# A mixing projection in which some rounded parts of the next operand are stored one or two products later

## The chip, the cores and the metric

The kernel runs on one core of one Trainium2 chip. The metric is the device time of one execution in microseconds (us). Work is spread over five engines, each with its own in-order list of instructions: TensorE (PE in the profile; PEld is its weight load), VectorE (DVE), ScalarE (ACT), GpSimd (POOL) and SyncE (SP). POOL and SP here mostly issue DMA transfers, each through a queue of its own. Times of single instructions are given from the start of the profiled span.

## The reference

One layer of a decoder trunk, 512 tokens by 2048 features, in float32. Cut to the part around the change:

```
merged = gc * conv_branch + ga * attn_branch
x = x + merged @ w_mix_out                  # mixing projection, 2048 x 2048
h = rmsnorm(x, g_mlp)                       # the second norm
u = square(relu(h @ w_ff1))                 # 2048 x 8192
x = x + u @ w_ff2                           # 8192 x 2048
out = rmsnorm(x, g_final)
```

## The kernel before

**How a product is made.** A float32 operand is rounded to a high half (`split`, line 111, ACT, into tile `th`) and a low half, which is the rest (line 114, DVE, into `tl`). Each of `th` and `tl` has two buffers. A product is then three passes on PE: high by high, low by high and high by low (lines 195, 197, 199 in `mm_rows` for the mixing projection, lines 171, 175, 177 in `mm_cols` for the MLP). One product is 16 + 8 + 16 + 8 = 48 matmuls in the mixing projection.

**Groups.** `w_mix_out` is worked through in four groups of 512 columns (g = 0 to 3, called first to fourth here), then `w_ff1` in sixteen groups, of which the first is `g0`. Each group is a two-by-two block product done with seven products instead of eight. They are named by the block or the sum of blocks of the left operand: A11, A12, S1, S3, S2, S4, A22. Sums and differences of weight blocks are made by DVE (line 128). Weights (tiles `x`) come by 1 MB loads (line 234): SP issues those of the mixing projection, POOL those of `g0`. The order of products is A11, A12, S1, S3, S2, S4, A22 in the first three groups (`head`, `tail2`) and A11, A12, S1, S2, S4, S3, A22 in the fourth (`tail3`). PE accumulates into banks a, b, c and d; ACT copies a bank out as it fills (`snap`, line 268, `o`) and DVE adds the others (`plus`, line 131).

**What follows a group.** Each group yields four quarters `o` of the new x. DVE adds the old x to a quarter (line 1372, tile `xr`), POOL stores it (line 1373, `x_d`), ACT sums its squares (line 532, `junk`), PE transposes it in four matmuls (line 1389, `ptr`), and ACT copies the transposed pieces, scaled by the gain, into `f` (line 1398). There is one pair of `f` tiles, which each group uses in turn; so a group can write it only when the group before it has stored what lies there.

**The five parts.** From the `f` of one group the kernel makes five pieces of the left operand of `w_ff1`: the sums S1, S2, S3 and S4 and the plain block A22. Each has the name of a product of the MLP that will read it; here they are called part S1 and so on. `Mix.give` calls `out`, which rounds one part: high half into one of two buffers `staged` (line 111, ACT), low half in place in `f` or `s` (line 114, DVE). POOL then stores both halves to DRAM (line 1414, `h_d`, 256 KB each). Blocks A11 and A12 take another way (`f_d`, line 1401); their halves are made by `split_part` after a load (line 1349) in one instruction of 1536 columns on ACT and one on DVE, tile `A`. Parts of the fourth group do not leave the core. Before `g0` needs them the stored parts are loaded again (line 1347, `S` and the last `A`, 1.5 MB each, on POOL).

**What sets the order.** A table, `after`, says behind which product of the running group each step for the group before it is written. The parts S2 and S4 are given at once when the sums are made (`sums`), S1, S3 and A22 by the table. The build then orders each engine's list from that; instructions marked to be kept in program order, the rounding and the stores of the parts among them, keep the order in which they were written. The lines of the table are 1527 to 1546:

```
        late = g == 1
        for n in ("A12", "S3") if late else ("A11", "S2" if g == 3 else "S1"):
            after.add(n, turn_waiting)
        after.add("A22", turn_first)
        if before:
            after.add("A12" if late else "A11", before.first_of, before.sums)
            for n, part in (("A12", "S1"), ("S1", "S3"), ("S2", "A22")):
                after.add(n, lambda before=before, part=part: before.give(part))
        ...
            after.add("S4", lambda: g0.ahead(0, 0))
            after.add("S4", lambda: split_part("A11"))
```

Of the kernel before, what the change touches and what calls it, by code (L numbers as in the profile page):

```python
# [45 lines left out]
def tile_hybrid_block(ctx: ExitStack, tc, x, g_mix, w_in, b_f, b_gate, conv_w, w_conv_out,  # L46
# [679 lines left out]
    part = stat.tile([P, 1], F32, tag="vf", name="part", bufs=4)  # L726
# [10 lines left out]
    A11, A12 = (Q1.cut(n, 0) for n in ("A11", "A12"))  # L737
# [24 lines left out]
    A11, A12 = (Q1.cut(n, 1) for n in ("A11", "A12"))  # L762
# [314 lines left out]
    n = 0  # L1077
# [252 lines left out]
    n = turns[0] + 1  # L1330
# [11 lines left out]
    def begin_part(n, k):  # L1342

        Q2[n] = pair(k, F32R, n).rearrange("p e (q s) -> p e q s", q=KT // 2)
        if n in SPLIT:
            tc.keep_in_program_order(
                nc.gpsimd.dma_start(out=Q2[n][:, :, :KT // 2 - 2].bitcast(F32), in_=h_d[:, SPLIT.index(n)]))
        else:
            nc.gpsimd.dma_start(out=Q2[n][:, 1, :KT // 2 - 2].bitcast(F32), in_=f_d[:, int(n == "A12")])

    def split_part(n):
        lo = Q2[n][:, 1, :KT // 2 - 2]
        split_in_order(lo.bitcast(F32), Q2[n][:, 0, :KT // 2 - 2], lo, kept=n)
# [164 lines left out]
    for g in range(4):  # L1518
        mix = mixes[g] = Mix(g)
        after = Steps()  # L1520
        if g == 0:
            for n, n2 in zip(("A11", "A12", "S1", "S3", "S2"), ("S1", "S3", "S2", "S4", "A22")):
                after.add(n, quads3[n2])
        if g == 3:
            after.add("S1", mix.fourth, lambda: begin_part("A12", 4))
# [3 lines that stand above are left out]
        after.add("A22", turn_first)  # L1529
        if before:  # L1530
            after.add("A12" if late else "A11", before.first_of, before.sums)
            for n, part in (("A12", "S1"), ("S1", "S3"), ("S2", "A22")):
                after.add(n, lambda before=before, part=part: before.give(part))
        if g < 3:
            after.add("S2", mix.fourth)
        else:
            after.add("A12", lambda: begin_part("A11", 0))
            after.add("S4", lambda: g0.ahead(0, 0))
            after.add("S4", lambda: split_part("A11"))
            after.add("S3", lambda: g0.ahead(1, 0))  # L1540
            after.add("A22", lambda: g0.ahead(0, 1))
            after.add("A22", lambda: split_part("A12"))
        group = groups[g]
        group.after = after
        if g == 0:
            after.add("A11", group.first_sum)
        if g == 3:
            group.mid["A22"] = turn_first
            group.freed = lambda: (g0.ahead(1, 1), begin_part("S1", 1))
        group.head(True, between=groups[1].first if g == 0 else lambda: None)  # L1550
        (group.tail2 if g < 3 else group.tail3)()
        before = mix
# [15 lines left out]
    def factors(common, r):  # L1568

        ms = const.tile([P, NT], F32, name="ms")  # L1570
        nc.vector.tensor_reduce(out=ms, in_=ss2, axis=AX.X, op=ALU.add)
        nc.gpsimd.tensor_tensor(out=r, in0=ms, in1=mhalf.to_broadcast([P, NT]), op=ALU.pow)
        ones = const.tile([P, P], F32, name="ones")
        nc.vector.memset(ones, 1.0 / S)
        pt = bank(6, "mean")
        nc.tensor.matmul(pt[:, :NT], ones, ms, start=True, stop=True)
        mean, back = (const.tile([P, 1], F32, name=n) for n in ("mean", "back"))
        nc.vector.tensor_reduce(out=mean, in_=pt[:, :NT], axis=AX.X, op=ALU.add)
        nc.gpsimd.tensor_tensor(out=common, in0=mean, in1=mhalf, op=ALU.pow)
        nc.vector.reciprocal(out=back, in_=common)  # L1580
        nc.vector.tensor_scalar(out=r, in0=r, scalar1=back, scalar2=None, op0=ALU.mult)
        nc.vector.tensor_tensor(out=r, in0=r, in1=r, op=ALU.mult)
# [5 lines left out]
                     A12=[in_order, lambda: mix.sums(False), lambda: factors(common, turned)])  # L1588
# [250 lines left out]
```

## Time and profile before

| | |
|---|---|
| time, median of 3 runs | 2417.17 us (2416.66 to 2418.52) |
| profiled execution, its own time | 2418.55 us |
| span in the profile | 2416.7 us |
| mean granted TensorE clock | 0.998 |
| PE busy | 2396.0 us, 99% of the span |
| DVE busy | 2029.8 us, 84% |
| ACT busy | 1205.1 us, 50% |
| POOL busy | 300.0 us, 12% |

A row of the timeline has the start, the length, the engine, the line, the operation, the tiles (out<-in, buffer numbers left out) and, in brackets, how long the engine stood idle before it and what ended that. The second group of the mixing projection runs from about 1059 to 1098 us, the fourth from about 1138 to 1181 us, and the first group of the MLP follows.

### The profile page before, as it was taken

What the parts mean: (1) busy time and instruction counts of PE and PEld (TensorE: products, weight loads), DVE (VectorE), ACT (ScalarE), POOL (GpSimd) and SP (SyncE); (2) the same over time, 40 slices, a digit from 0 to 9 for tenths busy, and PEclk for the clock granted to TensorE, in tenths of its full rate; (3) what the DMA queues carried; (4) which work ended last, traced back from release to release, by engine and by line L of the source; (5) the groups of instructions that cost most, each with busy time, mean ns of one, the idle gap of its engine ahead of it and who ended that gap; (6) DMA issues with size and microseconds to landing.
All of it is one profiled execution on the core that took longest, in us unless ns stands there. A gap on an engine that the chain in (4) does not pass through costs nothing.

```text
span 2416.7 us, 41351 instructions
## 1 busy us (share of the span) xinstructions
PE 2396.0 (99%) x17775; PEld 2259.7 (94%) x17775; DVE 2029.8 (84%) x1683; ACT 1205.1 (50%) x1238; POOL 300.0 (12%) x480
## 2 busy tenths in 40 slices
PE   9999999999999999999999999999999999999998
PEld 9999999999999999899999999999998888888886
DVE  7987677789888768888988889888887888889898
ACT  7444444445545534446665666666664333333334
POOL 1100111121111112023300000000011001100000
PEclk9999999999999999999999999999999999999999
DMA  8664444464565755566956564655678467665662
GB/s 276 187 189 153 150 154 153 153 205 152 178 201 181 259 176 202 179 193 224 324 184 225 199 231 170 224 206 198 233 288 292 168 210 252 218 212 183 232 231 100
DMA packets 279847, 491.98 MB, mean 204 GB/s; under 512 B 11820, under 2 KB 191112, under 8 KB 279280
## 3 DMA queue, kind: packets, MB, share of 16 engines
q1 hardware_dynamic: 226384, 272.71, 35.6%
q0 software_dynamic: 52672, 215.57, 24.4%
q8 instruction: 139, 2.28, 0.4%
q10 hardware_dynamic: 608, 1.06, 0.1%
q14 instruction: 44, 0.36, 0.0%
HBM read 379.70 MB, written 109.07 MB: 202 GB/s over the span
## 4 chain that ended last, share of the span: by engine, by line
PE 90%; DVE 3%; issue 2%; DMA 2%; ACT 1%; POOL 1%; SPq 0%; POOLq 0%; DVEq 0%; ACTq 0%
PE a L171 6%; PE a L175 6%; PE a L177 6%; PE d L171 5%; PE d L175 5%; PE d L177 5%; PE a L197 5%; PE a L195 5%; PE a L199 5%; PE c L177 4%; PE c L171 4%; PE c L175 4%; PE d L199 3%; PE d L195 3%; PE d L197 3%; PE b L171 3%
## 5 line engine op out<-in xcount | busy, mean ns | idle before, releaser
L111 ACT ACTIVATE th<-x 128x2048 fp32r<-128x2048 f32 (+1 forms) x280 | 537.0, 1918 | 486.6 <-DVE x L128 175.5
L114 DVE TENSOR_TENSOR tl<-x,th 128x2048 fp32r<-128x2048 f32 (+2 forms) x282 | 639.5, 2274 | 152.8 <-ACT th L111 149.1
L128 DVE TENSOR_TENSOR x<-x,x 128x2048 f32<-128x2048 f32 (+1 forms) x160 | 366.1, 2288 | 23.0 <-DMA x<-in_w_in_dram 17.6
L111 ACT ACTIVATE th<-y 128x2048 fp32r<-128x2048 f32 (+1 forms) x109 | 185.3, 1701 | 274.2 <-PE a L197 138.8
L114 DVE TENSOR_TENSOR tl<-y,th 128x2048 fp32r<-128x2048 f32 (+1 forms) x109 | 219.0, 2013 | 28.5 <-ACT th L111 28.1
L195 PE MATMUL a<-th,us 128*128 128x512 f32 x512 | 199.3, 389 | 0.4 <-ACT th L111 0.4
L197 PE MATMUL a<-th,us 128*128 128x512 f32 x512 | 199.2, 389 | 0.0
L171 PE MATMUL c<-S,th 128*128 128x256 f32 x848 | 195.9, 277 | 0.0
L175 PE MATMUL c<-S,th 128*128 128x256 f32 x848 | 195.7, 277 | 0.0
L171 PE MATMUL a<-S,th 128*128 128x256 f32 x784 | 182.3, 278 | 0.0
L175 PE MATMUL a<-S,th 128*128 128x256 f32 x784 | 180.7, 276 | 0.0
L171 PEld LDWEIGHTS c<-S,th 128*128 128x128 f32 x848 | 159.3, 188 | 0.0
L175 PEld LDWEIGHTS c<-S,th 128*128 128x128 f32 x848 | 159.3, 188 | 0.0
L171 PEld LDWEIGHTS a<-S,th 128*128 128x128 f32 x784 | 147.2, 188 | 0.6 <-issue 0.5
L175 PEld LDWEIGHTS a<-S,th 128*128 128x128 f32 x784 | 147.3, 188 | 0.5 <-issue 0.5
L199 PE MATMUL a<-tl,us 128*128 128x512 f32 x512 | 136.9, 389 | 0.6 <-DVE tl L114 0.6
L171 PE MATMUL b<-A,th 128*128 128x256 f32 x544 | 126.0, 277 | 1.4 <-ACT th L111 1.4
L171 PE MATMUL a<-A,th 128*128 128x256 f32 x544 | 126.5, 278 | 0.0
L171 PE MATMUL d<-S,th 128*128 128x256 f32 x544 | 126.4, 278 | 0.0
L175 PE MATMUL d<-S,th 128*128 128x256 f32 x544 | 125.7, 277 | 0.0
L171 PE MATMUL d<-A,th 128*128 128x256 f32 x544 | 125.7, 277 | 0.0
L175 PE MATMUL b<-A,th 128*128 128x256 f32 x544 | 125.5, 277 | 0.0
(401 smaller groups left out, 6030.7 us busy)
## 6 DMA issues: line engine op xcount, KB each, us to landing
x<-in_w_in_dram SPq DMA_DIRECT2D x86, 1024.0 KB, 5.9
y<-in_w_ff_dram SPq DMA_DIRECT2D x64, 1024.0 KB, 7.5
x<-in_w_ff_dram SPq DMA_DIRECT2D x60, 1024.0 KB, 8.2
us<-s_d POOLq DMA_DIRECT2D x48, 1024.0 KB, 9.2
s_d<-rh POOLq DMA_DIRECT2D x32, 896.0 KB, 5.4
s_d<-r POOLq DMA_DIRECT2D x32, 896.0 KB, 5.9
x<-in_w_mix_out_dram SPq DMA_DIRECT2D x17, 1024.0 KB, 6.9
g_d<-o POOLq DMA_DIRECT2D x32, 256.0 KB, 2.9
```

What stands on the lines that cost most here:

```text
L111: return tied(nc.scalar.activation(out=hi, in_=src, func=AF.Copy))
L114: return tied(nc.vector.tensor_tensor(out=lo, in0=src, in1=hi.bitcast(F32), op=ALU.subtract))
L128: return nc.vector.tensor_tensor(out=out, in0=a, in1=b, op=ALU.subtract)
L171: i = nc.tensor.matmul(o, hi[:, q, js], Sh, start=first and q == 0 and j == 0, stop=False, skip_group_check=True)
L175: nc.tensor.matmul(o, hi[:, q, js], Sl, start=False, stop=False, skip_group_check=True)
L177: i = nc.tensor.matmul(o, lo[:, q, js], Sh, start=False, stop=q == nq - 1, skip_group_check=True)
L195: tied(nc.tensor.matmul(o, Sh, hi[:, q, :], start=begin and q == 0, stop=False, skip_group_check=True))
L197: tied(nc.tensor.matmul(o, Sl, hi[:, q, :], start=False, stop=False, skip_group_check=True))
L199: tied(nc.tensor.matmul(o, Sh, lo[:, q, :], start=False, stop=q == nq - 1, skip_group_check=True))
```

## The change

The table gets an entry for each group. In the second group part S1 stays behind product A12, part S3 moves from behind product S1 to behind product S3, and part A22 from behind S2 to behind S4: one product later each, in that group's order. The third group keeps the old entry. In the fourth group, with its other order of products, part S1 moves from behind A12 to behind S2 (two products later), part S3 from behind S1 to behind S4 (two later), and part A22 from behind S2 to behind S4 (one later). So two parts move in the second group and three in the fourth. Nothing is computed differently, and no instruction or transfer is added or removed.

```
         if before:
             after.add("A12" if late else "A11", before.first_of, before.sums)
-            for n, part in (("A12", "S1"), ("S1", "S3"), ("S2", "A22")):
+            for n, part in {1: (("A12", "S1"), ("S3", "S3"), ("S4", "A22")), 2: (("A12", "S1"), ("S1", "S3"), ("S2", "A22")),
+                            3: (("S2", "S1"), ("S4", "S3"), ("S4", "A22"))}[g]:
                 after.add(n, lambda before=before, part=part: before.give(part))
```

What this does to the order of three lists, as the build makes them (`-` before, `+` now, a blank both; numbers in the names of weight tiles differ between the two builds where the tiles are the same).

ACT in the second group, around product A22, whose high half is `th<-x_11306`. The two `staged<-f` are the parts S3 and A22; `th<-x_11740` is the first operand of the third group.

```order
 L111 ACTIVATE staged<-s_11387 128x512
 L268 ACTIVATE o<-d 128x512
-L111 ACTIVATE staged<-f 128x512 x2
 L111 ACTIVATE th<-x_11306 128x2048
 L1398 ACTIVATE f<-ptr,cols 128x256 x2
-L268 ACTIVATE o<-a 128x512
+L111 ACTIVATE staged<-f 128x512
+L268 ACTIVATE o<-a 128x512
+L111 ACTIVATE staged<-f 128x512
 L111 ACTIVATE th<-x_11740 128x2048
```

The two roundings of parts stood ahead of the operand of A22 and now stand behind it, and behind the first copy into `f` of the group's own quarters.

ACT at the end of the fourth group, before. `th<-x_12392` is the operand of product S3, `th<-x_12229` that of A22, `th<-x_12590` that of the MLP's product A11; `A_12383` is the MLP's block A11, `A_12452` its A12.

```order
L111 ACTIVATE th<-x_12392 128x2048
L1394 ACTIVATE A_12383<-ptr,cols 128x256
L268 ACTIVATE o<-a 128x512
L111 ACTIVATE A_12383<-A_12383 128x1536
L1394 ACTIVATE A_12452<-ptr,cols 128x256
L1398 ACTIVATE f<-ptr,cols 128x256 x2
L111 ACTIVATE staged<-f 128x512
L268 ACTIVATE o<-c 128x512
L111 ACTIVATE th<-x_12229 128x2048
L532 ACTIVATE junk,ss_10795<-o 128x256 x2
L111 ACTIVATE th<-x_12590 128x2048
```

The same stretch of ACT now, from part S1 (`staged<-s`) on; `A_12378` is A11, `A_12447` is A12, `th<-x_12653` the operand of the MLP's product A12.

```order
L111 ACTIVATE staged<-s_12308 128x512
L111 ACTIVATE staged<-f 128x512
L268 ACTIVATE o<-c 128x512
L111 ACTIVATE th<-x_12590 128x2048
L111 ACTIVATE staged<-f 128x512
L111 ACTIVATE A_12378<-A_12378 128x1536
L532 ACTIVATE junk,ss_10795<-o 128x256 x2
L1394 ACTIVATE A_12378<-ptr,cols 128x256
L111 ACTIVATE th<-x_12653 128x2048
L1394 ACTIVATE A_12447<-ptr,cols 128x256
L1398 ACTIVATE f<-ptr,cols 128x256 x2
L111 ACTIVATE A_12447<-A_12447 128x1536
```

Three parts are now rounded here where one was, and the rounding of A11 has moved from ahead of three large operands to behind the last part.

POOL in the same place. `x_12653`, `x_12737` and `x_12741` are weights of the MLP's first group, 1 MB each.

```order
 L234 DMA x_12653<-in_w_ff_dram 128x8x256
-L1414 DMA h_d<-staged 128x512
-L1414 DMA h_d<-f 128x512
-L1373 DMA x_d<-o 128x2x256
 L234 DMA x_12737<-in_w_ff_dram 128x8x256
+L1414 DMA h_d<-staged 128x512 x2
+L1414 DMA h_d<-s_12308 128x512
+L1414 DMA h_d<-f 128x512
 L1373 DMA x_d<-o 128x2x256
 L234 DMA x_12741<-in_w_ff_dram 128x8x256
+L1414 DMA h_d<-staged 128x512
+L1414 DMA h_d<-f 128x512
```

The load of `x_12737` now goes ahead of all late stores, and the two stores of part A22 come behind the load of `x_12741`.

## The prediction

> **What bounds the kernel now.** I read the page first, then the waits of PE, then the timeline around each of them.
>
> ```profile
> PE 2396.0 (99%) x17775; PEld 2259.7 (94%) x17775; DVE 2029.8 (84%) x1683; ACT 1205.1 (50%) x1238; POOL 300.0 (12%) x480
> PE 90%; DVE 3%; issue 2%; DMA 2%; ACT 1%; POOL 1%; SPq 0%; POOLq 0%; DVEq 0%; ACTq 0%
> ...
> PE d L195 <- ACT th L111: 2.6, 1, 2.6
> PE c L195 <- ACT o L268: 1.0, 1, 1.0
> ```
>
> PE is busy 99% of the span and carries 90% of the chain. The two waits (sum, count, longest) are the largest that PE has from 1010 to 1260 us, the stretch that the change touches. So the change can win back 3.6 us of waiting, plus what hangs on it, and loses whatever new wait it gives PE. Both waits, with the products around the first:
>
> ```profile
> 1087.21 1.11 PE L199 MATMUL c<-tl,M 128*128 128x256 f32 x8
> 1090.95 0.39 PE L195 MATMUL d<-th,M 128*128 128x256 f32 x1 [2.64 <-ACT th L111]
> 1098.17 0.60 PE L1389 MATMUL ptr<-ident,o 128*128 128x128 f32 x4
> 1098.52 0.37 PE L195 MATMUL a<-th,M 128*128 128x256 f32 x1
> 1104.09 1.04 PE L1389 MATMUL ptr<-ident,o 128*128 128x128 f32 x8
> 1104.88 0.36 PE L195 MATMUL b<-th,M 128*128 128x256 f32 x1
> 1159.32 0.38 PE L195 MATMUL c<-th,M 128*128 128x256 f32 x1 [0.96 <-ACT o L268]
> ...
> 1089.00:1092.00 3.00, 1.04 (x9) 1.05 (x10) 1.76 (x2) 3.00 (x6) 1.08 (x2) 1.00 0.91 355
> 1092.00:1096.00 4.00, 4.00 (x23) 4.00 (x22) 3.96 (x4) 3.42 (x7) 0.71 (x1) 0.57 0.43 113
> 1096.00:1100.00 4.00, 4.00 (x37) 4.00 (x36) 4.00 (x4) 2.54 (x3) 0.00 (x0) 1.00 0.80 250
> ```
>
> In the last three rows (the core's busy times by engine, then granted clock, DMA share, GB/s) the clock is 0.57 in the 4 us after the wait and 1.00 around it: 0.43 x 4 = 1.7 us more are lost, 23 matmuls ran where 37 run next. The first wait thus costs 2.64 + 1.7 = 4.3 us. Why ACT is late for it:
>
> ```profile
> 1085.96 0.63 ACT L111 ACTIVATE staged<-f 128x512 fp32r<-128x512 f32 x1 [6.31 <-DMA h_d<-staged]
> 1088.47 0.63 ACT L111 ACTIVATE staged<-f 128x512 fp32r<-128x512 f32 x1 [1.89 <-DMA h_d<-staged]
> 1089.01 1.89 ACT L111 ACTIVATE th<-x 128x2048 fp32r<-128x2048 f32 x1
> 1090.81 0.82 ACT L1398 ACTIVATE f<-ptr,cols 128x256 f32<-128x256 f32 x2
> 1091.52 0.59 ACT L268 ACTIVATE o<-a 128x512 f32<-128x512 f32 x1
> 1092.00 1.92 ACT L111 ACTIVATE th<-x 128x2048 fp32r<-128x2048 f32 x1
> ```
>
> The parts S3 and A22 wait for a `staged` buffer, that is for stores to land, and the operand of product A22 stands behind them.
>
> **Step 1, second group: the wait goes.** The operand now stands ahead of both parts, in the 6.31 us that ACT idled, so PE can pass from S4 to A22 without a wait at about 1088.2. What could go here is 4.3 us.
>
> **Step 2, third group: most of it comes back.** Right behind that operand now stands the copy into `f` (line 1398), and `f` holds the low halves of parts S2 and S4 until they are stored. The later store:
>
> ```profile
> L1414 POOL DMA_DIRECT2D h_d<-f x1: 560/560/560, 1081.4 to 1081.4; - x1
> DMA to landing us min/median/max: 8.5/8.5/8.5
> ...
> 1094.47 2.29 DVE L114 TENSOR_TENSOR tl<-x,th 128x2048 fp32r<-128x2048 f32 x1
> 1102.88 0.69 DVE L1372 TENSOR_TENSOR o<-o,xr 128x512 f32<-128x512 f32 x1
> ```
>
> It lands at 1081.4 + 8.5 = 1089.9; the copy ran after that anyway before, now ACT stands until then. From there ACT does the copy (0.8), part S3 (0.6), the copy of bank a (0.5), part A22 (0.6) and the operand of the third group (1.9): 1094.3. It ended at 1093.9 before; DVE's half of it began at 1094.47 and can now begin at 1094.3. From there DVE has the same instructions back to back down to line 1372 at 1102.88, whose quarter PE must transpose before the third group's A12. So DVE is 0.2 us early, not 4.3: that quarter is ready at 1102.88 + 0.69 - 0.2 = 1103.4. PE comes to it much sooner: 1088.2 + 5.5 (A22; the next product took 1104.09 - 1098.52 = 5.6) + 0.35 (transposes) + 5.6 (A11) + about 0.5 of small waits for DVE + 0.35 (the first four transposes) = 1100.6. It waits 2.8 us and starts b near 1103.8, where it started at 1104.88: a gain of 1.1 us instead of 4.3. And a wait of 2.64 us cost 1.7 us of clock above. I take it that one of 2.8 us does so again: -1.1 + 1.7 = **+0.6**; without it, -1.1.
>
> [...]
>
> **Step 3, fourth group: half of the second wait goes.** Rows ahead of the copy that ends it:
>
> ```profile
> 1158.18 0.61 ACT L111 ACTIVATE staged<-s 128x512 fp32r<-128x512 f32 x1
> 1158.69 0.58 ACT L268 ACTIVATE o<-c 128x512 f32<-128x512 f32 x1
> ...
> 1170.43 1.93 ACT L111 ACTIVATE th<-x 128x2048 fp32r<-128x2048 f32 x1
> 1172.55 0.72 POOL L1373 DMA_DIRECT2D x_d<-o  x1 [0.77 <-DVE o L1372]
> 1168.58 1.75 DVE L114 TENSOR_TENSOR A<-A 128x1536 fp32r<-128x1536 f32 x1
> 1184.03 1.50 ACT L111 ACTIVATE A<-A 128x1536 fp32r<-128x1536 f32 x1
> 1181.08 0.37 PE L171 MATMUL a<-A,th 128*128 128x256 f32 x1
> 1187.15 0.30 PE L171 MATMUL b<-A,th 128*128 128x256 f32 x1
> ...
> L1414 POOL DMA_DIRECT2D h_d<-staged x1: 569/569/569, 1170.4 to 1170.4; - x1
> DMA to landing us min/median/max: 6.8/6.8/6.8
> h_d<-staged POOLq DMA_DIRECT2D x5, 256.0 KB, 4.0
> ...
> L234 POOL DMA_DIRECT2D x<-in_w_ff_dram x1: 904/904/904, 1177.8 to 1177.8; - x1
> DMA to landing us min/median/max: 9.3/9.3/9.3
> ```
>
> Part S1 is gone from ahead of the copy: 0.5 us earlier, and PE with it.
>
> **Step 4, the MLP's A11: a new wait.** A11's rounding lay under product S3 (DVE's half ended at 1170.3; PE reads it at 1181.08). Now part A22 and two operands stand ahead of it. The operand of product A22 (1170.43) no longer has the `f` copies (0.8), a part (0.6) and a bank's copy (0.6) ahead of it: it starts near 1168.4 and ends at 1170.3. Then come the `f` copies and part S1, whose store is issued at about 1171.7 and lands 4.0 (median of five) to 6.8 later (the one nearest in time), at 1175.7 to 1178.5. Only then has part A22 a buffer. After its rounding (0.6) DVE does its low half (0.7; so its stores are issued at 1177.0 to 1179.8), the MLP's first operand (2.3) and A11's low half (1.75), with A11's high half on ACT (1.5) beside that. The end is at 1181.1 to 1183.9; PE, 0.5 early, comes at 1180.6. The wait is 0.5 to 3.3 us, and it is a piece of the next sum.
>
> **Step 5, the MLP's A12: a second one.** The low half of part A22 lies in `f`; its store stands in POOL's queue behind a 1 MB load. That load stands in turn behind the `x_d` store of a quarter (at 1172.55 before), whose sum on DVE now has two parts' low halves (1.4) and an operand's (2.3) more ahead of it, less the 0.5 of step 3 and a little that DVE idled (not quoted; I take 0.25): about 1175.5. Such a load took 9.3 us before: 1184.8, plus 0.8 for each of the two stores (the load's 9.3 us less the 6.8 of a store is 2.5 us for 768 KB more), 1186.4. The copy of the last quarters into `f` waits for that, and behind the copy (0.8) stand A12's high half (1.5), on DVE its low half (1.75), line 1372 for the last quarter (0.7) and its transposes (0.35), in PE's list just behind the first matmul of A12. Sum 5.1: A12 goes on at 1191.5, where it stood at 1187.15: +4.35, with step 3 and the wait of step 4 inside. The lower end: if the queue has drained, the store takes the median 4.0 from its issue, at best 1177.0, and lands at 1181.0. Then A12 is ready at 1186.1, PE does not wait for it, and only step 4's 0.5 is left, which step 3 gives back: 0. So steps 3 to 5 together cost 0 to +4.35; I take **+2.5**, above the middle, since a 1 MB load does stand ahead of the store.
>
> **Sum.** +0.6 + 2.5 = +3.1 us. Against the profiled execution's own 2418.55 that is 2421.7; this execution lies 1.4 above the median of the runs shown, so on the median: 2417.17 + 3.1 = **2420.3 us**. Its own range, with both ends of steps 3 to 5: +0.6 to +4.95, 2417.8 to 2422.1. Behind this stretch PE waits for almost nothing, so what it has lost at 1190 us it keeps to the end. About 0.2% (4.8 us) is what a measurement can tell from no change; the forecast lies inside.
>
> **Rivals.**
>
> *No halved clock in step 2.* -1.1 + 2.5 = +1.4: 2418.6. For it: the 0.96 us wait halved nothing. Against: 2.64 us did. Chance 0.22. [...]
>
> *A second halved clock, at the MLP's A12.* PE waits there for A11, then within 6 us for A12 and the transposes, up to 4.9 us in all. If these fall together the clock halves once more: +3.1 + 1.7 = +4.8, and +6.65 at the upper ends: 2422 to 2423.8, slower. It decides from a wait of some 2.6 us in one piece, which the upper half of steps 4 and 5 gives. Chance 0.25.
>
> *The gain stays.* The store of step 2 lands as fast as one a little later did, ACT and DVE come 2.8 us sooner, and steps 4 and 5 find cover: -4.3 - 0.5 = -4.8, 2412.4.
>
> ```profile
> L1414 POOL DMA_DIRECT2D h_d<-f x1: 540/540/540, 1087.6 to 1087.6; - x1
> DMA to landing us min/median/max: 5.7/5.7/5.7
> ...
> 1100.00:1120.00 20.00, 20.00 (x175) 20.00 (x174) 19.73 (x18) 11.57 (x24) 8.71 (x14) 1.00 0.54 185
> ```
>
> Against it: nothing issued before that store changes, and DVE, busy 19.73 of the 20 us that follow, has no slack to catch up in. Chance 0.06.
>
> **How the numbers follow.** The forecast has 0.47. Slower by over 0.2% are most of the second halving and a tail of the forecast: 0.20 + 0.05 = 0.25. Faster by over 0.2%: the kept gain, 0.06. Within: 0.69. For 8 in 10 I go from 2414.5 (below the case without a halved clock by the spread of the runs, and some way to the kept gain) to 2425.0 (both halvings at the upper ends, 2423.8, and that spread).
>
> **What would show it.** Step 1: no wait of d at 1088. Step 2: line 1398 on ACT waiting to 1089.9 for `h_d<-f`, PE idle 2 to 3 us before the second transposes at 1103.4, and a clock below 1.00 in the 4 us after, or not. Step 3: the wait of c near 0.5. Step 4: PE waiting for `A` L114 at 1181. Step 5: ACT line 1398 idle for `h_d<-f` around 1183 to 1186 and PE idle before the transposes behind A12. I am wrong if PE does not wait at 1100, or if the two waits at the MLP are missing.

## The result: 0.2% slower

| | before | changed |
|---|---|---|
| time, median of 8 runs | 2418.04 us (2414.8 to 2420.24) | 2424.84 us (2422.28 to 2426.89) |
| ratio | 1 | 1.0024, 95% interval 1.0015 to 1.0033 |
| profiled execution's span | 2416.7 us | 2422.9 us |

The ratio is worth 5.8 us (3.6 to 8.0); the two medians are 6.8 us apart. The likeliest time on record was 2420.3, with a range of 2414.5 to 2425.0 and a chance of 0.25 for slower by over 0.2%: the time lies in the range, but only 0.2 us under its upper end, and above the 2422 to 2423.8 of the rival with a half clock at the MLP's A12.

**The waits of PE** from 1010 to 1260 us in the changed kernel (sum, times, longest, in us). Of the two waits shown before, the one for `th` is gone and the one of bank c has fallen from 1.0 to 0.6. In their place stand those that steps 2, 4 and 5 named: quarters of line 1372, A11 (`A L114`) and A12 (`A L111`).

```profile
PE ptr L1389 <- DVE o L1372: 4.8, 3, 2.5
PE b L164 <- ACT A L111: 0.7, 1, 0.7
PE c L195 <- ACT o L268: 0.6, 1, 0.6
PE a L175 <- DVE A L114: 0.5, 1, 0.5
```

**PE's timeline.** First two rows of the kernel before that the prediction did not show, the transposes ahead of the second group's b and a matmul of the MLP's bank d; then the changed kernel at these matmuls and at those of the prediction's rows.

```profile
1057.84 0.60 PE L1389 MATMUL ptr<-ident,o 128*128 128x128 f32 x4
1199.11 0.25 PE L164 MATMUL d<-S,th 128*128 128x192 f32 x1
```

```profile
1056.95 0.60 PE L1389 MATMUL ptr<-ident,o 128*128 128x128 f32 x4
1092.51 0.60 PE L1389 MATMUL ptr<-ident,o 128*128 128x128 f32 x4
1101.57 0.66 PE L1389 MATMUL ptr<-ident,o 128*128 128x128 f32 x4 [2.45 <-DVE o L1372]
1101.98 0.36 PE L195 MATMUL b<-th,M 128*128 128x256 f32 x1
1157.50 0.39 PE L195 MATMUL c<-th,M 128*128 128x256 f32 x1 [0.55 <-ACT o L268]
1180.81 0.39 PE L175 MATMUL a<-A,th 128*128 128x256 f32 x1 [0.53 <-DVE A L114]
1187.18 0.35 PE L164 MATMUL b<-A,th 128*128 128x192 f32 x1 [0.75 <-ACT A L111]
1189.58 1.12 PE L1389 MATMUL ptr<-ident,o 128*128 128x128 f32 x4 [2.04 <-DVE o L1372]
1203.96 0.25 PE L164 MATMUL d<-S,th 128*128 128x192 f32 x1
```

Subtract the rows of the same matmul. At 1057 us the changed kernel is 0.9 us ahead, where nothing differs yet: that is the scatter of single executions. At the transposes before the third group (1098.17 before) it is 5.7 ahead, so the missing wait gave 4.8. At the third group's b (1104.88 before) it is 2.9 ahead: the wait of 2.45 us has taken most of that back. At bank c (1159.32) it is 1.8 ahead, at the MLP's d (1199.11) 4.85 behind. From bank c in the fourth group to the MLP's d the changed kernel thus loses 6.7 us in this execution.

**ACT and the stores** behind these waits, in the changed kernel. The landing time of a transfer stands in the row below its issue.

```profile
1088.21 0.84 ACT L1398 ACTIVATE f<-ptr,cols 128x256 f32<-128x256 f32 x2 [5.97 <-DMA h_d<-f]
1184.91 0.84 ACT L1398 ACTIVATE f<-ptr,cols 128x256 f32<-128x256 f32 x2 [3.25 <-DMA h_d<-f]
...
L234 POOL DMA_DIRECT2D x<-in_w_ff_dram x1: 925/925/925, 1174.9 to 1174.9; - x1
DMA to landing us min/median/max: 8.7/8.7/8.7
...
L1414 POOL DMA_DIRECT2D h_d<-f x1: 555/555/555, 1177.2 to 1177.2; - x1
DMA to landing us min/median/max: 7.6/7.6/7.6
```

Both copies into `f` stand where the prediction put them, and for the store it named. The store of A22's low half lands at 1177.2 + 7.6 = 1184.8, 1.2 us behind the 1 MB load ahead of it (1174.9 + 8.7 = 1183.6).

**The clock.** PE's busy time (and matmuls) in stretches of 3.41 us of the changed kernel, then granted clock, DMA share, GB/s:

```profile
1096.46:1099.87 3.41, 2.66 (x24) 1.00 0.04 18
1099.87:1103.29 3.42, 1.72 (x15) 1.00 0.44 156
1185.21:1188.62 3.41, 1.57 (x12) 1.00 0.56 236
1188.62:1192.03 3.41, 2.45 (x12) 0.50 0.22 77
1192.03:1195.45 3.42, 3.42 (x18) 0.50 0.92 300
```

The wait of 2.45 us at 1100 halved nothing; the waits of 0.75 and 2.04 us at the MLP halved the clock for 6.83 us.

### The profile page after: what moved, and what is told of

It reads as the page before. It is cut to its first block, busy times and chain, and to the rows that moved or that the text cites. A ratio compares the mean times of both kernels' runs of the same rounds, so it can differ in the third digit from the quotient of the medians.

```text
span 2422.9 us, 41351 instructions
## 1 busy us (share of the span) xinstructions
PE 2399.9 (99%) x17775; PEld 2262.6 (93%) x17775; DVE 2029.7 (84%) x1683; ACT 1205.1 (50%) x1238; POOL 301.0 (12%) x480
## 4 chain that ended last, share of the span: by engine, by line
PE 90%; DMA 3%; DVE 3%; issue 2%; ACT 1%; POOL 1%; SPq 0%; POOLq 0%; DVEq 0%; ACTq 0%
PE a L171 6%; PE a L175 6%; PE a L177 6%; PE d L171 5%; PE d L175 5%; PE d L177 5%; PE a L199 5%; PE a L195 5%; PE a L197 5%; PE c L171 4%; PE c L175 4%; PE c L177 4%; PE d L195 3%; PE b L171 3%; PE d L197 3%; PE b L175 3%
## 5 line engine op out<-in xcount | busy, mean ns | idle before, releaser
L111 ACT ACTIVATE th<-x 128x2048 fp32r<-128x2048 f32 (+1 forms) x280 | 537.0, 1918 | 489.6 <-DVE x L128 174.3
L114 DVE TENSOR_TENSOR tl<-x,th 128x2048 fp32r<-128x2048 f32 (+2 forms) x282 | 639.7, 2274 | 157.0 <-ACT th L111 153.4
L111 ACT ACTIVATE th<-y 128x2048 fp32r<-128x2048 f32 (+1 forms) x109 | 185.4, 1701 | 273.2 <-PE a L197 138.8
L114 DVE TENSOR_TENSOR tl<-y,th 128x2048 fp32r<-128x2048 f32 (+1 forms) x109 | 219.1, 2014 | 28.7 <-ACT th L111 28.2
L171 PE MATMUL a<-A,th 128*128 128x256 f32 x544 | 126.6, 278 | 0.0
L171 PE MATMUL d<-S,th 128*128 128x256 f32 x544 | 126.3, 278 | 0.0
L175 PE MATMUL a<-A,th 128*128 128x256 f32 x544 | 125.5, 277 | 0.5 <-DVE A L114 0.5
```

The lines of the kernel that those rows point to most:

```text
L111: return tied(nc.scalar.activation(out=hi, in_=src, func=AF.Copy))
L114: return tied(nc.vector.tensor_tensor(out=lo, in0=src, in1=hi.bitcast(F32), op=ALU.subtract))
L171: i = nc.tensor.matmul(o, hi[:, q, js], Sh, start=first and q == 0 and j == 0, stop=False, skip_group_check=True)
L175: nc.tensor.matmul(o, hi[:, q, js], Sl, start=False, stop=False, skip_group_check=True)
```

## The experiments

Each experiment is timed against the kernel before, in five rounds on the same chip; e1 to e4, e5 to e8 and e9 to e12 ran on three different chips, so ratios are compared and not times. The times of one kernel scatter by some 5 to 12 us, so an interval of a ratio is about 0.2% wide, and the traces have to say what the times can't. To compare these I use two stretches of PE, each from one matmul to the same matmul in every kernel: from the transposes at 1057.84 to the third group's b at 1104.88 (47.0 us before), and from there to the MLP's d at 1199.11 (94.2 us before).

### Each group's entry alone

In this code and the next the entries are shortened: `changed` and `old` stand for them.

```
 e1: for n, part in {1: changed, 2: old, 3: old}[g]:
 e2: for n, part in {1: old, 2: old, 3: changed}[g]:
```

> Only the second group's entry of the table is changed; the fourth group keeps the old one. My theory, after the two traces: the wait of 2.64 us and its half clock go (4.7 us measured together), the wait for the third group's second quarter comes (2.45 us), so this part alone gains: about -2 us, 2415.5 to 2417 against 2418, without a half clock; about -0.3 if the new wait lies in one window of the clock. The last 1.3 us that the two traces differ by between 1104 and 1140 us (PE's pace, 2.83 against 2.72 us per half product) may or may not come again. Rival (the second group's entry is what costs, by the pace and by what comes later): +1 us or more.

> Only the fourth group's entry is changed. My theory: the whole loss lies here: -0.5 (bank c) + 0.5 (A11 late) + 0.75 and 2.0 (A12 and the last quarter late) + 1.7 to 2.9 (half clock) = +4.5 to +6, so 2422.5 to 2424; the trace must show ACT's copies into f waiting some 3 us for the store of A22's low half. Rival (the loss is shared with the second group or comes at the first rows of the second MLP product, 1810 us): +2 us or less.

Measured: the second group's entry alone 1.0000 (0.9990 to 1.0011), the fourth group's alone 1.0021 (1.0010 to 1.0031), 5.1 us. The loss is the fourth group's, as far as intervals of this width tell. In its trace ACT's copies wait as expected, though for 2.15 us and not 3:

```profile
1187.04 0.84 ACT L1398 ACTIVATE f<-ptr,cols 128x256 f32<-128x256 f32 x2 [2.15 <-DMA h_d<-f]
1184.05 0.39 PE L175 MATMUL a<-A,th 128*128 128x256 f32 x1 [1.36 <-DVE A L114]
1191.71 0.55 PE L1389 MATMUL ptr<-ident,o 128*128 128x128 f32 x3 [1.96 <-DVE o L1372]
```

The gain that I expected of the second group alone, 2 us, is not there. Its trace has the same 2.45 us of waiting, all of it in one stretch of 3.41 us (what the expectation calls a window of the clock; the last section has what the traces show of it), and here the clock halved:

```profile
1098.32:1101.73 3.41, 0.96 (x9) 1.00 0.41 150
1101.73:1105.14 3.41, 3.41 (x18) 0.50 0.59 214
```

### Parts of the fourth group's entry

```
 e3: 3: (("S1", "S3"), ("S2", "S1"), ("S2", "A22"))   # S1 moved
 e4: 3: (("A12", "S1"), ("S1", "S3"), ("S4", "A22"))  # A22 moved
 e7: 3: (("S1", "S3"), ("S2", "S1"), ("S4", "A22"))   # S1 and A22 moved
 e8: 3: (("S2", "S1"), ("S2", "A22"), ("S4", "S3"))   # all three, S3 last
```

> In the fourth group only part S1 moves, from behind A12 to behind S2; S3 stays behind S1 and A22 behind S2 (three roundings lie closer together then). My theory, in which the store of A22's low half decides: that store stands ahead of the third 1 MB load as before, so no wait at A12; bank c comes 0.5 us sooner: -0.5 to +0.7 us. Rival (three parts close together are too many for ACT, DVE and the two buffers, whatever the store): +3 us or more, with PE waiting for A11 or A12.

> In the fourth group only part A22 moves, from behind S2 to behind S4; S1 and S3 stay. By the order lists this puts its rounding ahead of A11's, and its stores ahead of the second and third 1 MB load: earlier, not later. My theory: its store lands sooner and nothing waits at A12, A11's rounding is 0.6 later in 10 us of slack: -0.3 to +0.5 us. Rival (any move of A22 to S4 costs): +3 us or more.

> Only the fourth group, with two of its three moves: S1 behind S2 and A22 behind S4, S3 stays behind S1. By the order lists A22 then needs no store to land first, and its two stores stand ahead of the third 1 MB load. My theory (what costs is the third part, which must wait for a buffer and then stores behind a load): -0.7 to +1 us against before. Rival (A22 behind S4 costs together with S1 behind S2): +4 us or more.

> Only the fourth group, with all three moved but in another order: S1 and A22 behind S2, S3 behind S4, so that S3 is the third part and its stores come behind a 1 MB load. My theory (it is the place of the third part, whichever it is): +4 to +6 us as with the change's own entry; ACT's copies into f wait for the store from f again. Rival (it is A22 that must not be last): 0 to +1 us.

Measured: 0.9997 (0.9987 to 1.0007), 1.0002 (0.9992 to 1.0012), 0.9999 (0.9990 to 1.0007) and 1.0013 (1.0004 to 1.0021). One part later, or two, cost nothing that shows. In e7 A22 needed no buffer to come free, and its store was issued early and held nobody:

```profile
L1414 POOL DMA_DIRECT2D h_d<-f x1: 542/542/542, 1172.2 to 1172.2; - x1
DMA to landing us min/median/max: 5.2/5.2/5.2
```

Three cost, with S3 last as with A22 last: in e8 the copies into `f` wait for a store again. The low halves of both lie in `f`; that of S1 lies in `s`, and S1 as the last of three was not tried. The cost is under the 4 to 6 us that I expected, though its interval reaches into them (3.1 us, 1.0 to 5.1); the wait is shorter too, 1.29 us:

```profile
1184.51 0.84 ACT L1398 ACTIVATE f<-ptr,cols 128x256 f32<-128x256 f32 x2 [1.29 <-DMA h_d<-f]
```

### The third part's store: another queue, or another place in the same

```
 e5, in out():
-    nc.gpsimd.dma_start(out=h_d[...], in_=o)
+    (nc.sync if g == 2 and n == "A22" else nc.gpsimd).dma_start(out=h_d[...], in_=o)
 e9, with stored[0] the last store of a part:
-group.freed = lambda: (g0.ahead(1, 1), begin_part("S1", 1))
+def behind_stores():
+    with tc.issue_after(stored[0].ins):
+        g0.ahead(1, 1)
+        begin_part("S1", 1)
```

Both start from the changed kernel.

> The changed kernel, but the two stores of the fourth group's part A22 are issued by SP, whose queue is empty there, in place of POOL, where they stood behind a 1 MB load. My theory (the place in POOL's queue makes the store land at 1184.9): it lands 4 to 6 us after its issue at 1177.2, so at 1181 to 1183; the copies into f stop waiting by 2 to 4 us, PE's waits at A12 and for the last quarter (0.75 and 2.0 us) and their half clock go; the wait for A11 stays. 3 to 5 us less than the change: 2419.5 to 2421.5. Rival (the DMA engines are full, 0.97 to 1.01 of their time from 1170 to 1184 us, and the queue does not matter): it lands near 1184 all the same, 1 us less or nothing.

> The changed kernel, but the fourth 1 MB load of the MLP's first group and the load of S1's reloaded halves (1.5 MB) are issued by POOL behind the stores of part A22, not ahead of them. My theory (the store is late because 1 MB stands ahead of it in its own queue, which lands in order): the store from f lands near 1181, 3 to 4 us sooner; the copies into f run at 1181.7 without a wait; PE's wait for A12 (0.75 us) and for the last quarter (2.0 us) go, and with them the half clock there (2.9 us lost in the profile of the change): 3 to 5.5 us less than the change, 2419.5 to 2422. The wait for A11 (0.5 us) stays. Rival (the DMA engines are full whatever the order, as the store by SP landed even later): it lands at 1184 or later, 1 us less or nothing.

Measured: the store by SP 1.0037 (1.0025 to 1.0049), slower still by 3 to 4 us; the load behind the stores 1.0007 (0.9998 to 1.0016), so 2.9 to 4.1 us less than the changed kernel's 1.0019 and 1.0024. In both cases the intervals overlap, so the traces have to carry it. The store by SP, then that of e9:

```profile
L1414 SPq DMA_DIRECT2D h_d<-f x1: 545/545/545, 1176.8 to 1176.8; - x1
DMA to landing us min/median/max: 10.7/10.7/10.7
```

```profile
L1414 POOL DMA_DIRECT2D h_d<-f x1: 560/560/560, 1179.6 to 1179.6; - x1
DMA to landing us min/median/max: 2.9/2.9/2.9
```

Issued 2.8 us later than by SP, the store of e9 lands 5 us earlier (1182.5 against 1187.5). In SP's queue only the part's other store of 256 KB stood ahead of it, issued at 1176.1, but the load of 1 MB in POOL's queue, issued at 1174.6, was under way, and 1.5 MB were issued there 0.3 us after it. SP's queue was not the slower one elsewhere: its 1 MB loads `x<-in_w_ff_dram` took 8.3 us in the changed kernel (median of 60), those of POOL 9.3 (`us<-s_d`, median of 48). So here an empty queue was no short cut while another had megabytes under way: my expectation of e5 was wrong, and its rival came nearer, though the store was not as late as in POOL's queue but later. With e9 this says for this store: it is late because of the megabytes that are under way with it (7.6 us to landing in the changed kernel, 10.7 in e5), and issuing it ahead of them is what helps (2.9 us in e9). With the load behind the stores ACT's wait is gone, as is PE's for A12 and the last quarter; what is left in that place is the wait for A11, longer than in the changed kernel (0.53 and 0.72 us):

```profile
1182.72 0.39 PE L175 MATMUL a<-A,th 128*128 128x256 f32 x1 [1.60 <-DVE A L114]
```

### A11's rounding ahead of the parts

```
+if g == 3:
+    after.add("S4", lambda: split_part("A11"))   # ahead of the parts
 if before:
 ...
-    after.add("S4", lambda: split_part("A11"))
```

e6 has this in the changed kernel, e10 in e9.

> The changed kernel, but A11's rounding is written ahead of the parts S3 and A22 behind product S4, so ACT and DVE do it under product A22 and not behind the last part. My theory (the copies into f, held by the store of A22's low half, cost most; A11's place is a small piece): PE's wait for A11 (0.5 us in the profile of the change, 1.4 in that of the fourth group alone) goes, the later ones stay: 0.5 to 1.5 us less than the change, 2423 to 2424.5. Rival (A11's late rounding holds up all that follows on ACT and DVE): 4 us less, about 2420.

> The last kernel, and A11's rounding is written ahead of the parts S3 and A22 besides. If the two waits at the MLP (for A11 and for A12 with the last quarter) are the whole loss, both are gone and what is left is the second group's part (0 to -2 us) and bank c (-0.4): -2.5 to +0.5 us against before, at or below the kernel before. Rival (something else in the fourth group's entry costs too): +2 us or more with no wait of PE over 0.5 us between 1176 and 1200.

Measured: 1.0023 (1.0013 to 1.0034) and 1.0017 (1.0008 to 1.0026). In neither does PE wait for A11, and neither is faster for it. In e6 PE comes to A12 earlier and waits there for what it saved:

```profile
1187.43 0.36 PE L164 MATMUL b<-A,th 128*128 128x192 f32 x1 [1.61 <-ACT A L111]
1189.22 0.39 PE L175 MATMUL b<-A,th 128*128 128x256 f32 x1 [1.30 <-DVE A L114]
```

In e10 both waits are gone, but bank c waits 1.37 us, and a new wait is there, for the reloaded halves of S1, whose load had been put behind the stores:

```profile
1195.33 0.36 PE L171 MATMUL c<-S,th 128*128 128x256 f32 x1 [1.76 <-DMA S<-h_d]
...
L1347 POOL DMA_DIRECT2D S<-h_d x1: 717/717/717, 1181.0 to 1181.0; - x1
DMA to landing us min/median/max: 14.2/14.2/14.2
```

My expectation for e10 had no place for this wait, and its account of the loss was too short: what is put behind the stores is late in its turn. In e9 PE waits 0.36 us for the same halves and goes on at 1195.17, here at 1195.33: both kernels are held by this load, so taking away e9's wait for A11 could gain nothing. The time of e10 is no better than that of e9; its second stretch (below) is the same length.

### What costs nothing, together; and the change once more

```
 e11: {1: changed, 2: old, 3: (("S1", "S3"), ("S2", "S1"), ("S2", "A22"))}
```

> The second group's entry as changed, and in the fourth group only S1 moved: the two pieces that cost nothing alone. They should add: 0 and -0.7, so -2.5 to +1 us against before; PE's waits in the profile: some 2.5 us for the third group's second quarter, 0.3 for bank c, none at the MLP. Rival: they disturb each other, +2 us or more.

> The changed kernel once more, unaltered. My theory (the waits belong to the order of the instructions, the half clock to where a wait falls in a 3.41 us grid that runs on by itself): the waits of 2 to 2.5 us for the third group's second quarter and of 2 to 3.5 us in all at A11, A12 and the last quarter come again within 0.7 us each; the half clock may come at the first, at the second, at both or at neither, as the 3.41 us stretch that holds the wait has more or less than some 1.9 us of it; the times +4 to +7 us against before. Rival (the waits themselves are chance): one of the two is missing or twice as long.

Measured: 0.9995 (0.9986 to 1.0005), so the pieces add to nothing; and for the change again 1.0019 (1.0009 to 1.0029), 4.6 us. The second trace of the change has three of the waits again, within 0.2 us; those for bank c and for A12 (0.55 and 0.75 us in the first) it does not have, and it has no half clock in either place:

```profile
1102.86 0.66 PE L1389 MATMUL ptr<-ident,o 128*128 128x128 f32 x4 [2.45 <-DVE o L1372]
1180.87 0.39 PE L175 MATMUL a<-A,th 128*128 128x256 f32 x1 [0.72 <-DVE A L114]
1189.01 0.66 PE L1389 MATMUL ptr<-ident,o 128*128 128x128 f32 x4 [2.04 <-DVE o L1372]
...
1098.90:1102.32 3.42, 1.51 (x14) 1.00 0.24 92
1187.65:1191.06 3.41, 2.05 (x18) 1.00 0.16 57
```

### The two stretches in all traces

In us, from the start of the same matmuls; an asterisk marks a stretch with a half clock in it.

| kernel | second group's entry | first stretch | fourth group's entry | second stretch |
|---|---|---|---|---|
| before | old | 47.0* | old | 94.2 |
| e3 | old | 43.6 | S1 moved | 95.0 |
| e4 | old | 45.0 | A22 moved | 95.1 |
| e7 | old | 45.1 | S1, A22 moved | 95.0 |
| e8 | old | 44.7 | three moved, S3 last | 97.1 |
| e2 | old | 46.5 | changed | 97.4 |
| e1 | changed | 45.0 | old | 95.2* |
| e11 | changed | 46.9 | S1 moved | 96.4* |
| changed | changed | 45.0 | changed | 102.0* |
| e12 | changed | 46.2 | changed | 97.5 |
| e6 | changed | 46.7 | changed, A11 ahead | 97.8 |
| e5 | changed | 45.1 | changed, store by SP | 104.3* |
| e9 | changed | 46.2 | changed, load behind | 97.6* |
| e10 | changed | 46.2 | both of these | 97.6 |

In e1, e5, e9 and e11 a half clock that the wait in the first stretch set off falls, for the most part, into the second (in e5 besides the one at the MLP). Half of that part is lost (in e1 18 matmuls ran in 3.41 us at the half clock, 31 or 32 in as long a stretch at full clock): without it the second stretch would be some 93.6 in e1 and 94.6 in e11. The first stretch takes 43.6 to 46.5 us with the old order and no half clock (mean 45.0 of five), 45.0 to 46.9 with the new (mean 45.9 of eight). The second takes 94.2 to 95.1 with at most two parts moved and no half clock, 97.1 to 97.8 with three moved, over 100 where the clock halves at the MLP. Of this PE stands idle for 0.6 to 1.5 us with at most two parts moved, for 2.9 to 4.2 with three (e8, e12, e2 and the changed kernel), and for 2.2 in e9.

From the second stretch to the end of the span it is 1217.6 us before (2416.7 - 1199.11), 1218.9 and 1223.8 in the two traces of the change, and 1216.8 to 1223.8 in all fourteen. With at most two parts moved the mean is 1219.5, with three 1219.7. So the loss does not lie there, but much of the scatter does. A part of that is PE's wait for an operand near 1810 us, at the start of the product with `w_ff2` (before, then changed):

```profile
PE a L195 <- ACT th L111: 0.4, 1, 0.4
PE a L195 <- ACT th L111: 2.2, 1, 2.2
```

It is 2.2 us in e1 too, which has the old entry of the fourth group, and 0.3 in e9, which has the new one. In the changed kernel, e1 and e4 it halves the clock (mean granted clock of the span 0.997, 0.997 and 0.998); in e8, e10 and e12, where it is 2.2 us too, it does not (0.999).

## Why the prediction was right, and where its sizes were off

**Step 1, the wait goes: right, its worth was not.** The operand of A22 is early and no wait for it is left in any trace with the new order. But the 4.3 us were those of one execution, and that is the luck of the trace that I read. With the same old order the wait for `th` was 3.0 us in e2, 0.9 in e3, 1.6 in e4, 1.2 in e7 and 1.5 in e8, and none of these halved the clock. The kernel before, as profiled, was the slowest of six in this stretch. Steps 1 and 2 together came to -1.1 or +0.6 us on record; the mean traces give +0.9 against the executions without a half clock (45.9 - 45.0) and the times of e1 0 (-2.4 to +2.7).

**Step 2, most of it comes back: right.** ACT stood 5.97 us for the store that I named, which landed at 1080.5 + 7.6 = 1088.1 (the forecast would be 1089.0 in this execution, which is 0.9 us ahead), DVE brought line 1372 late, and PE waited 2.45 us for 2.8 forecast (the times listed in that step add up to 1100.5, not 1100.6, which makes it 2.9). The half clock, put into the sum after one wait of 2.64 us had shown it, does not always come: it came with this wait in e1, e5, e9 and e11 and not in the changed kernel, e6, e10 and e12.

**Step 3: met in this trace, not shown as an effect.** Bank c waits 0.55 us, about 0.5 was forecast. But this wait scatters with either entry: 0.2 us in e1 and 0.96 before with the old one, none in e12 and 1.37 in e10 with the new. That the size was met is luck.

**Steps 4 and 5: right, and the size held without the half clock.** A11 came 0.5 to 1.4 us late (0.53, 0.72, 1.36; forecast 0.5 to 3.3), the copies into `f` waited for the store of A22's low half, and PE for the last quarter (2.04, 2.04, 1.96), for A12 only in the first trace of the change. (In the order lists the rounding of A11 has moved behind two large operands that stood behind it, those of A22 and of the MLP's A11, and not three; step 4 counts two.) In place of +2.5 us (0 to +4.35) the second stretch shows 97.4 and 97.5 against a mean of 94.8 in the four traces with at most two parts moved and no half clock: +2.6. In the first trace of the change the clock halved besides, and there it is +7.2. That rival was priced at 1.7 us of clock; the clock stayed half for 6.83 us, not 3.41. The wait for the last quarter lay on both sides of the start of the half clock there (1188.62; the last section has these borders), as in e5 (1190.42), the other trace with 6.83. The half clock lost 2.9 us there (half of the 2.45 us of work in its first 3.41 us, and half of the whole second).

**The sum.** +3.1 us was forecast, 5.8 and 4.6 measured, above and just inside the case's own range (+0.6 to +4.95). Without any half clock the traces give +0.9 and +2.6, together +3.5. The first of these is what the waits say: 2.45 us have come in place of a mean of 1.6 (the five waits of step 1 without a half clock). So two terms were mis-sized: the wait that goes, 4.3 us on record; and the half clock with its place, counted in full at step 2, where it comes in four of eight traces, and left to a rival at the MLP, where two of five traces have it (the changed kernel and e5 have it, e2, e6 and e12 don't). In the sum of steps 1 and 2 the two errors cancelled in part, and that the forecast lies near +3.5 is luck to this extent. As an estimate from these shares, and one of six for the old order, the half clocks add 1.7 x 4/8 + 2.9 x 2/5 - 1.7 x 1/6 = 1.7 us: 5.2 in all. The runs do not show this last part: 3.5 lies within the interval of the second measurement (2.2 to 7.0) and just under that of the first (3.6 to 8.0). The difference of single executions would not have shown any of it: the trace before held the one unlucky first wait of six.

**Behind the stretch: wrong.** The prediction has PE wait for almost nothing there. The wait near 1810 us is 2.2 us in both traces of the change, with a half clock in the first; but as far as fourteen executions tell it does not go with the entries (e1 and e9 above).

**The rivals.** That ACT's wait, and PE's behind it, lie with one store is shown by e9: with two loads put behind the stores, and nothing else, these waits are gone; the time falls to 1.0007, with an interval that overlaps the changed kernel's. Its second stretch (97.6, with 1.2 us of half clock) is no shorter than those of e12 and e2, as the wait for A11 and S1's load hold PE there; so how much of the loss the store alone makes is not shown. What is shown by e3, e4, e7, e8 and e2 is that the loss comes with the third part. That the gain does not stay (rival at 0.06) is shown by e1. No half clock in step 2 (rival at 0.22) is what both traces of the change have there, and the second half clock (0.25) is in the first of them. What else remains argued is how often the clock halves at each place; five or eight traces do not give a share.

## What to carry to other kernels

A wait that is removed is worth what it costs on average, not what it cost in the profile at hand: look for a store or a load that ends it, and expect its length to vary: here the wait for `th` took 0.9 to 3.0 us with the same order of the second group. Before a step is moved later, follow what its buffers hold up: here a low half stored in place held the next writer of the same tile (ACT, for 3.25 us in the changed kernel), and three parts in two buffers put the last one behind a megabyte. Taking a transfer to an empty queue did not help here while the transfers of another were under way (10.7 us to landing for 7.6); issuing it ahead of them did (2.9 us), and then the one put behind was the next to be late (14.2 us).

## What the runs showed that I had not expected

**In these traces the half clock keeps to a grid.** While PE still has work it lasts 3.41 us in the kernel before and at 1813 us in the changed kernel, and 6.83 us at the MLP. Where a trace has two such stretches, their starts differ by whole multiples of 3.4133 us: 1188.62 and 1813.26 in the changed kernel (183 of them), 1101.73 and 1808.29 in e1 (207), 1101.68 and 1190.42 in e5 (26). Cut along this grid, a stretch in which PE was busy 1.38 us or less was followed by a half clock each time (1.38 us before, 1.20 ahead of 1813 us in the changed kernel, 0.96 in e1 and e11, 0.36 in e5):

```profile
1088.91:1092.33 3.42, 1.38 (x12) 1.00 0.88 345
1092.33:1095.74 3.41, 3.41 (x18) 0.50 0.38 92
```

That is the kernel before. Here is e2, whose longer wait of 3.0 us lay across the border of two stretches and cost no clock:

```profile
1088.20:1091.61 3.41, 1.79 (x16) 1.00 1.06 395
1091.61:1095.02 3.41, 2.08 (x16) 1.00 0.61 236
```

With 1.57 us of work the clock halved in the changed kernel (shown above), with 1.51 it did not in e12, nor with 1.52 in e5 (from 1811.65 us on). So my estimate from these stretches is that the point lies near 1.4 to 1.6 us of work in 3.41: 2.04 us of idle time (before) and 1.84 us (changed) halved the clock. A wait of 2 to 3 us halved it here or not by where it fell: 2.64 us did (before), 3.0 did not (e2), and 2.45 did in e1 and did not in the changed kernel, where it was shared by two stretches with 2.66 and 1.72 us of work.

**In these traces PE has two paces at full clock.** The eight low-half matmuls of line 199 end each half of a product, so the distance of two such rows is a half product's time. In the changed kernel, before and after the wait at 1100:

```profile
1083.44 1.07 PE L199 MATMUL c<-tl,M 128*128 128x256 f32 x8
1086.16 1.07 PE L199 MATMUL c<-tl,M 128*128 128x256 f32 x8
...
1103.95 1.10 PE L199 MATMUL b<-tl,M 128*128 128x256 f32 x8
1106.78 1.10 PE L199 MATMUL b<-tl,M 128*128 128x256 f32 x8
```

That is 2.72 and 2.83 us, 4% apart, with the clock at 1.00 in both. In this stretch a pace mostly lasts until a wait or a transpose (in the changed kernel 94 matmuls in a row at the slower one from 1102.18 us on, behind the wait), and how much of either there is differs between executions of the same kernel: of PE's 17775 matmuls 2153 start 117 to 119 ns after the one before them in the first trace of the change, and 2867 in the second (the fast pace has 113 or 114). At 4.5 ns more each (2.83 - 2.72 us over 24) that is an estimated 10 and 13 us. What sets the pace I did not find; by this estimate it is one source of the scatter in the times.
